# RWKV-7 and gated DeltaNet step: the right merge products of an item and the left ones of the next, at one place and in one PSUM bank

## The chip, the core and the metric

The kernel runs on one core of one Trainium2 chip. Five engines work side by side, each through its own queue in order: PE (TensorE, matrix products, with its weight loads shown apart as PEld), DVE (VectorE), ACT (ScalarE), POOL (GpSimd) and SP, which here only issues transfers. The metric is the time of one execution on the device in microseconds (us); lower is better. Before the change it is 2265.62 us, the median of three runs (2259.42 to 2267.38).

## The reference

One inference step of a trunk of two layers, for one prompt of 1024 tokens (16 learned tokens are put ahead of it) and eight samples of 8 tokens each: 1104 tokens of width 1024. The first layer is a gated DeltaNet, the second an RWKV-7 time mixing, which is what the change concerns:

```python
def rwkv_mixer(xn, S0, shift_prev, mu, w_rkvz, w0, w1, w2, a0, a1, a2, k_k, k_a, r_k, lnx_w, lnx_b, w_o):
    ...
    rkvz = jnp.einsum('sbtd,sde->sbte', xs[:4], w_rkvz)
    ...
    def step(S, inp):
        r_t, k_t, v_t, d_t, kk_t, b_t = inp
        S = (S * d_t[:, :, None, :]
             + jnp.einsum('bhvk,bhk->bhv', S, -kk_t)[..., None] * b_t[:, :, None, :]
             + v_t[..., None] * k_t[:, :, None, :])
        return S, jnp.einsum('bhvk,bhk->bhv', S, r_t)
    ...
    return y @ w_o, S, xn[:, -1]
```

The kernel does not go token by token. It takes chunks of 64 tokens, and what the tokens of a chunk do to each other becomes a triangular system of 64 x 64 for each chunk and head, whose inverse is worked out ahead of the recurrence.

## The kernel before

The program runs in this order: projections, convolution and recurrence of the first layer; its output projection; for the second layer the keys and decays; then the stage of this change (about 1520 to 1820 us of the profile), in which PE works out the projections r, v and z while the triangular inverses of all chunks are made beside it; and last the "wave", the RWKV recurrence over time with the output projection filled in.

**The projections** (`projections` in `layer1`) set the clock of the stage. They are 24 output tiles in segments of 384, 384 and 336 tokens. Each product of 128 x 128 weights (split in two, `whi` and `wlo`) with a stretch of tokens (`xa`, `xc`, `xh`, `xl`) goes into the PSUM tile `d`. After every 8 products the generator yields; one such step is called a tick here, u = 0, 1, 2 and so on. A finished tile is copied out by ACT (`ev`) and sent to memory (`rvd`, `zd`).

**The inverses** (`inverse_plan`). An item n (0 to 23) is a pair of heads in one of three segments, six chunks each. The items are taken in five groups b: 4, 5, 5, 5 and 5 of them. For an item:

- `prepare`: ACT forms two exponentials in the item's loaded tile `sldcak` (L62 on `sldcak`), DVE multiplies (L1321, L1327), POOL too (L1326). The next item's tile is loaded by SP (L1265); there are two such tiles, so a load waits until the item before has been used by `lower`.
- `lower`: PE makes 24 small products `fL` and 4 sums `frss`; ACT copies them to `sGD` (L1344) and `L` (L1346).

For a group, `chain` works on DVE: a transposition of `sGD` to `invA` (L1370), 31 steps of two instructions each (L1292 and L1294), which invert all 32 x 32 diagonal blocks at once, and two transpositions of the result, to `T1n` (L1377) and to `sTD` (L1378). Then the blocks are merged: for each item q of the group 12 left products give Y = (lower block) x `T1n` in PSUM (`mY`), ACT copies them to `invY` (two copies, L485), 12 right products give Y x `sTD` (`mU`), and ACT writes them with a minus sign back to `sTD` (two activations, L62). `store` sends the group's `sTD` to memory (`ttd`, L1393 and L1395). Both PSUM tiles carry the tag "m", of which there is one buffer, a bank: a new tile waits until the last one has been copied out.

**What sets the order.** Inside this stage PE's order is written out by hand: a table `plan` says which function runs at which tick. `lower` of item n stands at tick LOWER[n]; the five chains are pumped up to END[b]; item q of group b has its left products at END[b] + 4 + 4q and its right ones two ticks later; the store follows the last item. At one tick merges come before `lower`. The other engines' queues are ordered by the framework's scheduler from its own estimate of times, so that a change in PE's order can also move instructions on ACT, DVE, POOL and SP.

Of the kernel before, what the change touches and what calls it, by code (L numbers as in the profile page):

```python
# [10 lines left out]
AF = mybir.ActivationFunctionType  # L11
# [24 lines left out]
class Builder:  # L36
# [438 lines left out]

    def merge_left(self, L21, T1n, pool):

        p = self.ps("m", 1, "Y")
        v = p[:, 0:192].rearrange("p (c i) -> p c i", i=32)
        for c in range(6):  # L480
            for a in (0, 64):
                self.mm(v[a + 32:a + 64, c, :], L21[a:a + 32, c, :], T1n[a:a + 32, c, :])
        Y = self.t(pool, [128, 192], "invY", 2).rearrange("p (c i) -> p c i", i=32)
        for a in (32, 96):
            self.nc.scalar.copy(Y[a:a + 32], v[a:a + 32])  # L485
        return Y

    def merge_right(self, Y, TT):

        p = self.ps("m", 1, "U")  # L490
        v = p[:, 0:192].rearrange("p (c i) -> p c i", i=32)
        for c in range(6):
            for a in (0, 64):
                self.mm(v[a:a + 32, c, :], Y[a + 32:a + 64, c, :], TT[a + 32:a + 64, c, 0, :])
        for a in (0, 64):
            self.act(TT[a:a + 32, :, 1, :], v[a:a + 32], AF.Identity, scale=-1.0)

# [805 lines left out]
    def inverse_plan(self, pool):  # L1303

        nc, t = self.nc, self.t
        keep = {}
        GD, TD = self.GD, self.TD
# [72 lines left out]

        def left(b, q):
            C = slice(6 * q, 6 * q + 6)
            keep["Y", b, q] = self.merge_left(self.L21[b % 2][:, C], keep["T", b][:, C], pool)

        def right(b, q):
            self.merge_right(keep.pop(("Y", b, q)), TD[:, 6 * q:6 * q + 6])

# [8 lines left out]


        return prepare, lower, chain, left, right, store


# [521 lines left out]
    def layer1(self, ctx, right, stay, xa, xb, x):  # L1922

        nc, tc = self.nc, self.tc
        pool = lambda n, c: c.enter_context(tc.tile_pool(name=n, bufs=1, reuse_waits="tile"))
# [43 lines left out]
        ip = pool("rinv", ctx)  # L1969
        self.rwkv_masks(ip, True)  # L1970
        prepare, lower, chain, first_, second_, store = self.inverse_plan(ip)
        plan = {}
        at = lambda u, f, *a: plan.setdefault(u, []).append((f, a))
        LOWER = (13, 19, 25, 31, 35, 41, 47, 53, 59, 63, 69, 76, 82, 88, 92, 98, 104, 110, 116, 120, 126, 132, 137, 142)
        DUR, END = (0,), (52, 88, 112, 137, 164)
# [8 lines left out]
        for b in range(5):  # L1984
# [10 lines left out]
            for q in range(len(items)):  # L1995
                at(END[b] + 4 + 4 * q, first_, b, q)
                at(END[b] + 4 + 4 * q + 2, second_, b, q)
            at(END[b] + 4 + 4 * q + 1 + 2, store, b, items)
# [229 lines left out]
```

## Time and profile before

| | |
|---|---|
| median of three runs | 2265.62 us (2259.42 to 2267.38) |
| span of the profiled execution | 2250.2 us; the page gives no separate time for that execution |
| distance of the three times from that span | 9.2, 15.4 and 17.2 us |
| PE, PEld busy | 94%, 86% of the span |
| DVE, ACT, POOL busy | 69%, 57%, 41% |
| PE's granted clock, mean | 0.980 of full speed |
| merge products in the profile | 576 passes of `mY`, 576 of `mU`, first at 1566.4 us, last at 1817.4 us |
| copies behind them | 48 of 0.31 us (`invY`), 48 of 0.32 us (`sTD`) |

How to read the lines that follow: a row of the time order has the start in us from the span's start, the duration, the engine, the source line, the operation, out<-in, the shape and the count; in brackets stands how long the engine was idle before it and what ended that. `x24` behind 12 products is right, since each of them runs as two passes. PE's duration includes the time in which a product drains, so neighbouring products overlap, and the distance between two starts says what a product costs.

### The profile page before, as it was taken

The numbers are of one execution on the slowest core, as the hardware profiler recorded it, in microseconds if no ns is written. First come the engines' busy times: TensorE is split into PE (matmuls) and PEld (weight loads), VectorE is DVE, ScalarE is ACT, GpSimd is POOL, SyncE is SP. The second block draws the span as 40 slices with busy tenths as digits, with TensorE's granted clock in tenths as the row PEclk, the third lists the DMA queues.
The fourth block names the chain that finished last, engine by engine and source line by source line (L and its number), as shares of the span: only waits on it lengthen the run. The fifth ranks groups of instructions, "written<-read, shape, count | busy, mean of one in ns | idle before, by whom it ended". The sixth has DMA issues, their size and how long they took to land. (4 is left out here: it accounts for less than half of the span.)

```text
span 2250.2 us, 55173 instructions
## 1 busy us (share of the span) xinstructions
PE 2119.2 (94%) x20452; PEld 1933.2 (86%) x20452; DVE 1552.8 (69%) x4229; ACT 1272.4 (57%) x3641; POOL 915.7 (41%) x1253
## 2 busy tenths in 40 slices
PE   6999999999999999999999999989999999999997
PEld 5888898889898888989898999988888988888876
DVE  6778759586776859577434585766977647866755
ACT  5545556565555546556633365663745446677774
POOL 3444344453433435353323154343523344444444
PEclk9999999999999999999999999989999999999998
DMA  4333232433433233333516215645556376677754
GB/s 118 94 87 106 74 104 67 103 88 90 112 90 85 75 99 94 94 103 102 180 42 172 83 46 180 212 164 177 157 172 169 109 212 168 184 216 231 232 177 134
DMA packets 430662, 292.66 MB, mean 130 GB/s; under 512 B 147145, under 2 KB 412986, under 8 KB 430394
## 3 DMA queue, kind: packets, MB, share of 16 engines
q1 hardware_dynamic: 430394, 289.14, 44.8%
q8 instruction: 161, 2.64, 0.5%
q14 instruction: 107, 0.88, 0.1%
HBM read 197.68 MB, written 91.37 MB: 128 GB/s over the span
## 5 line engine op out<-in xcount | busy, mean ns | idle before, releaser
L90 POOL TENSOR_TENSOR wlo<-wraw,whi 128x512 fp32r<-128x512 f32 (+1 forms) x246 | 324.5, 1322 | 369.4 <-ACT whi L86 342.5
L76 PE MATMUL d<-xc,whi 128*128 128x384 f32 (+2 forms) x1006 | 282.5, 339 | 0.2 <-ACT whi L86 0.2
L86 ACT CAST whi<-wraw 128x512 fp32r<-128x512 f32 (+1 forms) x246 | 150.0, 613 | 132.4 <-PE dq L76 50.7
L435 DVE SCALAR_TENSOR_TENSOR cvy<-raw,cw,cvy 128x408 f32<-128x408 f32 (+2 forms) x288 | 180.5, 640 | 16.5 <-ACT cvy L62 14.6
L76 PEld LDWEIGHTS d<-xc,whi 128*128 128x128 f32 (+1 forms) x1006 | 183.7, 189 | 3.7 <-issue 1.4
L76 PE MATMUL d<-xc,wlo 128*128 128x384 f32 (+3 forms) x476 | 158.6, 342 | 2.2 <-POOL wlo L90 2.2
L76 PE MATMUL dz<-xc,whi 128*128 128x384 f32 (+1 forms) x480 | 149.3, 342 | 0.0
L76 PE MATMUL d<-xa,whi 128*128 128x384 f32 (+3 forms) x450 | 144.5, 345 | 3.7 <-ACT ev L2028 3.5
L76 PE MATMUL dv<-xc,whi 128*128 128x384 f32 (+1 forms) x480 | 146.7, 334 | 0.0
L835 POOL TENSOR_SCALAR Sb<-Sb,eglb 128x128 f32<-128x128 f32 x128 | 82.5, 663 | 87.7 <-DMA Sb<-in_state_gdn 51.2
L76 PE MATMUL dz<-xa,whi 128*128 128x384 f32 (+1 forms) x288 | 100.5, 349 | 0.0
L471 DVE TENSOR_TENSOR invtmp<-invA,invT 72x31 f32<-72x31 f32 (+15 forms) x248 | 95.5, 385 | 7.0 <-DMA invA<-ltd 4.2
L76 PE MATMUL dv<-xa,whi 128*128 128x384 f32 (+1 forms) x288 | 100.1, 348 | 0.1
L473 DVE TENSOR_TENSOR invT<-invT,invtmp 72x31 f32<-72x31 f32 (+15 forms) x248 | 96.9, 391 | 2.8
L76 PEld LDWEIGHTS d<-xc,wlo 128*128 128x128 f32 (+1 forms) x476 | 89.6, 190 | 6.2 <-POOL wlo L90 2.8
L76 PEld LDWEIGHTS d<-xa,whi 128*128 128x128 f32 (+1 forms) x450 | 85.4, 192 | 7.0 <-ACT ev L2028 3.8
L76 PEld LDWEIGHTS dz<-xc,whi 128*128 128x128 f32 x480 | 89.6, 192 | 0.8
L76 PEld LDWEIGHTS dv<-xc,whi 128*128 128x128 f32 x480 | 88.5, 188 | 0.5 <-issue 0.4
L62 ACT ACTIVATE o<-rA,gcol 128x128 f32<-128x128 f32 x128 | 46.6, 372 | 72.7 <-DVE S L746 72.1
L76 PE MATMUL d<-xa,wlo 128*128 128x384 f32 (+3 forms) x252 | 86.1, 342 | 1.1 <-POOL wlo L90 1.1
L62 ACT ACTIVATE attn<-attn,gcol 128x128 f32<-128x128 f32 x144 | 46.5, 390 | 71.1 <-POOL attn L546 71.0
L62 ACT ACTIVATE raw<-cvy 128x408 f32<-128x408 f32 (+2 forms) x96 | 47.3, 512 | 54.5 <-DVE cvy L435 53.6
(522 smaller groups left out, 7036.1 us busy)
## 6 DMA issues: line engine op xcount, KB each, us to landing
wraw<-in_gdn_w_in SPq DMA_DIRECT2D x96, 256.0 KB
wraw<-in_rwkv_w_rkvz SPq DMA_DIRECT2D x80, 256.0 KB
Sb<-in_state_gdn SPq DMA_DIRECT2D x64, 256.0 KB
sldcak<-cakd SPq DMA_DIRECT2D x24, 576.0 KB
wraw<-in_rwkv_w_o SPq DMA_DIRECT2D x42, 256.0 KB
E<-drow SPq DMA_DIRECT2D x24, 384.0 KB
attn<-drow SPq DMA_DIRECT2D x24, 384.0 KB
wraw<-in_gdn_w_out SPq DMA_DIRECT2D x36, 256.0 KB
```

The lines of the kernel that those rows point to most:

```text
L62: return self.nc.scalar.activation(out, in_, func, bias=bias, scale=scale, **kw)
L76: self.nc.tensor.matmul(out, lhsT, rhs, start=start, stop=stop)
L86: nc.scalar.copy(hi, x)
L90: e.tensor_tensor(lo, x, hi.bitcast(F32), op=ALU.subtract)
L435: nc.vector.scalar_tensor_tensor(y[:, 0:wd], raw[:, k:k + wd], cw[k], y[:, 0:wd], op0=ALU.mult, op1=ALU.add)
L471: nc.vector.tensor_tensor(tmp, A[:, j, j + 1:32].unsqueeze(2).broadcast_to([nb, n, m]), Tv[:, j, 0:m].unsqueeze(1).broadcast_to([nb, n, m] ...
L473: nc.vector.tensor_tensor(Tv[:, j + 1:32, 0:m], Tv[:, j + 1:32, 0:m], tmp, op=ALU.subtract)
L835: nc.gpsimd.tensor_scalar(Sb[:, u], Sb[:, u], self.eglb[:, hv, 4 * g + u:4 * g + u + 1], None, op0=ALU.mult)
```

## The change

The functions `left` and `right` of the plan become one function, `merges`, which stands at END[b] + 4 + 4q. It takes one PSUM tile (`mYU`), lets PE make the right products of item q - 1 and then the left products of item q into it, each on the partitions that it had before, copies `invY`, and last copies the right products to `sTD`. The first place of a group has only left products. The last right products keep their tick, two behind the last left ones, as does the store. A group of five items uses six PSUM tiles instead of ten.

```diff
-    def merge_left(self, L21, T1n, pool):
-
-        p = self.ps("m", 1, "Y")
-        v = p[:, 0:192].rearrange("p (c i) -> p c i", i=32)
+    def merge_view(self, p):
+
+        return p[:, 0:192].rearrange("p (c i) -> p c i", i=32)
+
+    def merge_left(self, L21, T1n, v, pool):
+
         for c in range(6):
             for a in (0, 64):
                 self.mm(v[a + 32:a + 64, c, :], L21[a:a + 32, c, :], T1n[a:a + 32, c, :])
...
-    def merge_right(self, Y, TT):
-
-        p = self.ps("m", 1, "U")
-        v = p[:, 0:192].rearrange("p (c i) -> p c i", i=32)
+    def merge_right(self, Y, TT, v):
+
         for c in range(6):
             for a in (0, 64):
                 self.mm(v[a:a + 32, c, :], Y[a + 32:a + 64, c, :], TT[a + 32:a + 64, c, 0, :])
-        for a in (0, 64):
-            self.act(TT[a:a + 32, :, 1, :], v[a:a + 32], AF.Identity, scale=-1.0)
+        return lambda: [self.act(TT[a:a + 32, :, 1, :], v[a:a + 32], AF.Identity, scale=-1.0) for a in (0, 64)]
...
-        def left(b, q):
-            C = slice(6 * q, 6 * q + 6)
-            keep["Y", b, q] = self.merge_left(self.L21[b % 2][:, C], keep["T", b][:, C], pool)
-
-        def right(b, q):
-            self.merge_right(keep.pop(("Y", b, q)), TD[:, 6 * q:6 * q + 6])
+        def merges(b, q, items):
+
+            v = self.merge_view(self.ps("m", 1, "YU"))
+            after = None
+            if q:
+                after = self.merge_right(keep.pop(("Y", b, q - 1)), TD[:, 6 * q - 6:6 * q], v)
+            if q < items:
+                C = slice(6 * q, 6 * q + 6)
+                keep["Y", b, q] = self.merge_left(self.L21[b % 2][:, C], keep["T", b][:, C], v, pool)
+            if after:
+                after()
...
             for q in range(len(items)):
-                at(END[b] + 4 + 4 * q, first_, b, q)
-                at(END[b] + 4 + 4 * q + 2, second_, b, q)
+                at(END[b] + 4 + 4 * q, merges, b, q, len(items))
+            at(END[b] + 4 + 4 * q + 2, merges, b, q + 1, len(items))
             at(END[b] + 4 + 4 * q + 1 + 2, store, b, items)
```

What it does to the order is seen on PE first, in group 0, between the first left products and the second ones. `d_19665` is the projection tile that PE is at, `frss` the end of `lower` of item 8. Before, with the rows from the last projection products ahead of the right products to the second left ones:

```order
L76 MATMUL d_19665<-xc_107,wlo_19549 128x384
L76 MATMUL d_19665<-xc_107,whi_19548 128x384 x2
L76 MATMUL mU_19682<-sTD_18465,invY_19662 32x32 x12
L76 MATMUL d_19665<-xc_107,wlo_19549 128x384
...
L76 MATMUL frss_19741<-ssq_19612,hones_17015 32x192 x4
L76 MATMUL d_19749<-xa_103,whi_19399 128x336
...
L76 MATMUL d_19749<-xc_107,wlo_19400 128x336
L76 MATMUL mY_19758<-T1n_19525,L_3276_18466 32x32 x12
```

and with the change:

```order
L76 MATMUL d_19665<-xc_107,wlo_19549 128x384
L76 MATMUL d_19665<-xc_107,whi_19548 128x384 x2
L76 MATMUL d_19665<-xc_107,wlo_19549 128x384
...
L76 MATMUL frss_19726<-ssq_19612,hones_17015 32x192 x4
L76 MATMUL d_19734<-xa_103,whi_19399 128x336
...
L76 MATMUL d_19734<-xc_107,wlo_19400 128x336
L76 MATMUL mYU_19743<-sTD_18465,invY_19662 32x32 x12
L76 MATMUL mYU_19743<-T1n_19525,L_3276_18466 32x32 x12
```

The right products of item 0 moved behind `lower` of item 8, to the left products of item 1. The same place on ACT, before:

```order
L485 COPY invY_19662<-mY_19649 32x192 x2
L62 ACTIVATE sTD_18465<-mU_19682 32x6x32 x2
L2028 COPY ev_19705<-d_19665 128x384
L1344 COPY sGD_18464<-fL_19713 128x32x6
L1346 COPY L_3277_18467<-fL_19713 32x192 x2
L62 ACTIVATE ssq_19778<-sldcak_19610 128x384
L485 COPY invY_19771<-mY_19758 32x192 x2
```

and with the change:

```order
L487 COPY invY_19662<-mYU_19649 32x192 x2
L2032 COPY ev_19690<-d_19665 128x384
L1343 COPY sGD_18464<-fL_19698 128x32x6
L1345 COPY L_3277_18467<-fL_19698 32x192 x2
L62 ACTIVATE ssq_19777<-sldcak_19610 128x384
L487 COPY invY_19768<-mYU_19743 32x192 x2
L62 ACTIVATE sTD_18465<-mYU_19743 32x6x32 x2
```

The two activations to `sTD` left the space between `invY` and `sGD` and now stand behind the next `invY`. In group 2, ACT ahead of and behind the second left products (`sldcak_21437`, with the change `sldcak_21430`, is the loaded tile of the same item), before:

```order
L62 ACTIVATE sldcak_21437<-sldcak_21437 128x383
L62 ACTIVATE sldcak_21437<-sldcak_21437 128x384
L62 ACTIVATE sTD_18465<-mU_21469 32x6x32 x2
L2028 COPY ev_21504<-d_21426 128x384
L485 COPY invY_21537<-mY_21524 32x192 x2
L1344 COPY sGD_18464<-fL_21546 128x32x6
```

and with the change:

```order
L62 ACTIVATE sldcak_21430<-sldcak_21430 128x383
L62 ACTIVATE sldcak_21430<-sldcak_21430 128x384
L2032 COPY ev_21482<-d_21419 128x384
L487 COPY invY_21527<-mYU_21502 32x192 x2
L62 ACTIVATE sTD_18465<-mYU_21502 32x6x32 x2
L1343 COPY sGD_18464<-fL_21538 128x32x6
```

The exponentials stay where they were; the copies of the first right products, which stood right behind them and ahead of the second left products' `invY`, now stand behind that `invY`, since their products moved there too. On DVE the steps of group 1's inverse and the token mixes (`mixs`) that run among them are interleaved in another order over some 90 rows; apart from that, DVE, POOL and SP change the places of single neighbouring rows. Behind this stage the order of all engines is as before.

4 lines of the change are left out of this document (2 added, 2 removed).

## The prediction

> **What bounds the kernel now.** I read the page first (TensorE, PE, is busy for 94% of the span), then the waits of PE between 1560 and 1830 us, the stretch in which the merges run, then the order of time around the longest of them, and last the busy time by stretch. "<- X" is what the wait ended with; the three numbers are us in total, times, longest us.
>
> ```profile
> PE 2119.2 (94%) x20452; PEld 1933.2 (86%) x20452; DVE 1552.8 (69%) x4229; ACT 1272.4 (57%) x3641; POOL 915.7 (41%) x1253
> ```
> ```profile
> PE mU L76 <- ACT invY L485: 4.0, 4, 2.5
> PE fL L76 <- DVE sldcak L1327: 3.6, 1, 3.6
> PE mY L76 <- ACT sTD L62: 2.8, 2, 2.1
> PE fL L76 <- issue: 2.2, 1, 2.2
> ```
> A right product (mU) waits 4.0 us in all for the copy of the left product (invY), a left product (mY) 2.8 us for the copy that frees the bank (sTD). These 6.8 us are what the change can reach. The other two, at fL, are waits for VectorE (DVE): they are where a faster PE would only wait longer.
>
> The longest merge wait, in order of time (start, us, engine):
>
> ```profile
> 1566.36 0.57 PE L76 MATMUL mY<-T1n,L 32*32 32x32 f32 x24
> 1566.86 0.45 PE L76 MATMUL d<-xa,whi 128*128 128x384 f32 x1
> 1570.15 1.08 ACT L62 ACTIVATE sldcak<-sldcak 128x383 f32<-128x383 f32 x2 [6.24 <-DVE sldcak L1327]
> 1571.75 0.63 ACT L485 COPY invY<-mY 32x192 f32<-32x192 f32 x2
> 1572.44 0.57 PE L76 MATMUL mU<-sTD,invY 32*32 32x32 f32 x24 [2.53 <-ACT invY L485]
> 1575.02 0.52 PE L76 MATMUL d<-xa,wlo 128*128 128x384 f32 x1
> 1575.34 0.52 PE L76 MATMUL d<-xa,whi 128*128 128x384 f32 x1
> 1575.79 1.03 PE L76 MATMUL fL<-sldcak 64*32 64x64 f32 x45
> 1575.90 0.48 ACT L2028 COPY ev<-d 128x384 f32<-128x384 f32 x1 [2.19 <-PE d L76]
> 1576.96 0.32 ACT L1344 COPY sGD<-fL 128x192 f32<-128x192 f32 x1 [0.59 <-PE fL L76]
> 1577.32 1.25 DVE L1370 STREAM_TRANSPOSE invA<-sGD 128x1024 f32<-128x1024 f32 x1 [6.06 <-ACT sGD L1344]
> ```
> The copy waits in ACT's queue behind an exponential that waits for DVE; the right product stands 16 projection products behind the left one, and PE is there first. After the wait the products start every 0.32 us. Behind them stands fL, and DVE has been idle for 6.06 us when fL's copy lets it begin the next chain. From there DVE is the bound (columns of the next fence: stretch, its length, then busy time of PE, PEld, DVE, ACT, POOL, then PE's clock):
>
> ```profile
> 1572.93:1577.14 4.21, 4.21 (x71) 3.46 (x65) 0.00 (x0) 1.30 (x4) 0.00 (x0) 0.60 0.05 18
> 1577.00:1641.00 64.00, 56.77 (x718) 50.97 (x712) 61.68 (x128) 48.80 (x119) 34.79 (x36) 1.00 0.55 166
> 1715.00:1740.00 25.00, 22.82 (x314) 20.58 (x312) 21.84 (x44) 16.87 (x43) 9.62 (x12) 1.00 0.68 160
> 1744.00:1785.00 41.00, 41.00 (x417) 38.44 (x416) 35.96 (x89) 21.50 (x52) 17.17 (x14) 1.00 0.33 102
> ```
> ```profile
> 1641.31 1.35 PE L76 MATMUL fL<-sldcak 64*32 64x64 f32 x45 [3.59 <-DVE sldcak L1327]
> ```
> From 1577 to 1641 DVE is busy for 61.68 of 64 us and PE then waits 3.59 us for it; from 1744 on PE has no gap.
>
> **The change part by part.** It adds and removes no product and no copy: 24 items with 12 left and 12 right products each (the profile counts two passes to a product, 24 to a group), and four copies to an item. It does three things.
>
> *It gives each copy four ticks instead of two* (a tick is 8 projection products). A right product of every item but a group's last now stands 32 products behind its left one, and the bank is needed again after as long.
>
> *It removes stops.* A quiet stop of the last group:
>
> ```profile
> 1809.29 0.52 PE L76 MATMUL d<-xc,whi 128*128 128x384 f32 x2
> 1809.64 0.34 PE L76 MATMUL d<-xc,wlo 128*128 128x384 f32 x1
> 1809.82 0.33 PE L76 MATMUL d<-xc,whi 128*128 128x384 f32 x1
> 1810.08 0.57 PE L76 MATMUL mU<-sTD,invY 32*32 32x32 f32 x24
> 1810.58 0.44 PE L76 MATMUL d<-xc,whi 128*128 128x384 f32 x1
> 1810.86 0.33 PE L76 MATMUL d<-xc,wlo 128*128 128x384 f32 x1
> ```
> From 1809.82 to 1810.86 are two steps of d, 0.175 each when undisturbed (two products from 1809.29 to 1809.64), and the stop: 1.04 - 0.35 = 0.69 us. A second group of 24 passes behind the first costs at most 0.50 (1810.08 to 1810.58) and at least 0.40 (the row's 0.57 less its last pass of 0.19, over 23 steps, times 24). So a removed stop saves 0.19 to 0.29; I take 0.24, the middle. Counted in the order of work, places where fL stands at the same tick counted once, groups 0, 1 and 2 lose 3 stops each, groups 3 and 4 lose 4 each.
>
> *It moves the copies on ACT* into fours (two invY, two sTD). These are the same 1.28 us, and the next stop asks for them 5.6 us (32 x 0.175) later.
>
> Term 1, group 0. Without mU at 1572.44, fL comes after 24 products: 1566.86 + 0.10 (the first step is longer, as at 1810.58) + 24 x 0.175 + 0.09 = 1571.25 instead of 1575.79, 4.5 us earlier. On ACT invY still ends at 1572.38, a copy of d (0.48) follows, then sGD at 1572.86: 4.1 us earlier than 1576.96. DVE is free by then, so its chain begins 4.1 us earlier, and being 96% busy it reaches L1327 and fL at 1641.31 4.1 us earlier. What PE gains besides in group 0 (0.83 at 1590.94, below, and 3 stops) only lengthens the wait at 1641: nothing. **4.1 us.**
>
> The clock bears on this term: the granted clock was 0.60 in the 4.2 us behind a wait of 2.53 us, which made 8 products cost 8 x (0.32 - 0.175) = 1.2 us more. The Trainium skill (TensorE: Matmul & The Clock Gate, Part 1) has the clock halve after an idle window of about 3.4 us; by it a wait of 2.5 us would cost nothing further, term 1 would be 1.2 smaller and the whole about 8.9. The trace shows the slow products, so the row decides.
>
> The other waits that fall away:
>
> ```profile
> 1590.94 0.57 PE L76 MATMUL mU<-sTD,invY 32*32 32x32 f32 x24 [0.83 <-ACT invY L485]
> 1662.07 0.57 PE L76 MATMUL mU<-sTD,invY 32*32 32x32 f32 x24 [0.54 <-ACT invY L485]
> 1694.79 1.08 ACT L62 ACTIVATE sldcak<-sldcak 128x383 f32<-128x383 f32 x2 [5.02 <-DMA sldcak<-cakd]
> 1696.61 0.57 PE L76 MATMUL mY<-T1n,L 32*32 32x32 f32 x24 [2.09 <-ACT sTD L62]
> 1705.13 0.57 PE L76 MATMUL mY<-T1n,L 32*32 32x32 f32 x24 [0.69 <-ACT sTD L62]
> ```
> Term 2, group 1: 0.54 + 3 x 0.24 = **1.3 us**; DVE is not what PE waits for between 1642 and 1696.
>
> Term 3, group 2: 2.09 + 0.69 + 3 x 0.24 = 3.5 us on PE. The wait at 1696.61 is ACT held for 5.02 us by a load; with the change the bank was freed before it. But PE then meets DVE again:
>
> ```profile
> 1703.64 0.56 DVE L1321 TENSOR_TENSOR sldcak<-sldcak 128x383 f32<-128x383 f32 x1 [0.71 <-ACT sldcak L62]
> 1712.49 0.56 DVE L1327 TENSOR_TENSOR sldcak<-sldcak 128x384 f32<-128x384 f32 x1 [0.26 <-POOL sldcak L1326]
> 1715.18 0.56 DVE L1321 TENSOR_TENSOR sldcak<-sldcak 128x383 f32<-128x383 f32 x1 [1.34 <-ACT sldcak L62]
> 1740.20 1.35 PE L76 MATMUL fL<-sldcak 64*32 64x64 f32 x45 [2.23 <-issue]
> ```
> DVE's idle time on that way, which an earlier fL (through the load that fL releases) can close, is 0.71 + 0.26 + 1.34 = 2.3 us up to 1715, and behind it at most the 25 - 21.84 = 3.2 us of the window. So between 2.3 and 3.5 come through; I take **3.0 us**.
>
> Term 4, groups 3 and 4: 8 x 0.24 = 1.9 us, less what the last inverse holds back:
>
> ```profile
> 1782.68 2.11 DVE L1377 STREAM_TRANSPOSE T1n<-invT 128x1024 f32<-128x1024 f32 x1
> 1785.60 0.57 PE L76 MATMUL mY<-T1n,L 32*32 32x32 f32 x24
> ```
> T1n ends at 1784.79, 0.8 us ahead of mY; group 3's four stops bring PE 0.96 earlier. DVE has 5 us of idle time in that window and follows in part; I take off 0.2. **1.7 us.**
>
> Sum: 4.1 + 1.3 + 3.0 + 1.7 = 10.1. The profiled span would go from 2250.2 to about 2240. The three times lie 9.2 to 17.2 above the span, their median 15.4; that distance does not change. Forecast: 2265.6 - 10 = **2255.6 us**. What follows after 1820 begins with loads and products that these stops release, so I carry the 10 us to the end whole.
>
> **The rivals.**
>
> *Bank held too long (slower).* A group's last right product still stands 16 products behind the last left one, and now it also asks for the bank, which waits for two sTD copies more. If these copies end later than 2.8 us (16 x 0.175) after the stop, PE waits there, and it decides if it is as at 1572.44: 2.53 + 1.2 of slow clock + some 0.2, 3.9 us, in five groups 19.5. Less the 10: 2275. The tightest such place:
>
> ```profile
> 1596.86 0.63 ACT L485 COPY invY<-mY 32x192 f32<-32x192 f32 x2
> 1598.93 0.57 PE L76 MATMUL mU<-sTD,invY 32*32 32x32 f32 x24
> ```
> invY ends at 1597.49, two more copies at 1598.14, still 0.8 us early; and this place lies in DVE's stretch, where it costs nothing. Chance 0.05.
>
> *The stops save nothing.* Right products use the array's rows from 32 and 96, left ones from 0 and 64. If the array drains between them, the joint place costs two stops, and terms 2 to 4 lose 14 x 0.24 = 3.4: 2259. For it: every change from d to a group shows such a gap. Against it: within a group the passes already alternate between two row places in one bank, 0.0165 us apart. The Trainium skill (TensorEngine Tiling (Array Packing), Gotcha 1: PSUM Pressure) says that different row tiles cannot use one PSUM bank at once, which speaks for a wait between the two halves; the alternating passes do not show it. Chance 0.17.
>
> *DVE's stretch does not follow.* Its 128 rows lean on ACT (48.80 of 64 us busy), and the order of both is new there; four copies in a row can hold an operand of DVE for 0.65 us more at each of group 0's three joint places, and another interleaving of inverse and mixes can lose one more. Term 1 falls to about 1: 2258.7. Chance 0.16.
>
> *DVE follows further.* If it closes 4.5 instead of 3.0 us before 1740, PE's wait there falls from 2.23 + 3.5 - 3.0 = 2.7 to 1.2, and the slow clock behind it, 1.2 as above, goes too: 2265.6 - 12.8 = 2252.8. For it: 2.3 + 3.2 us of idle time. Against: part of that is DVE and ACT waiting for each other. Chance 0.17.
>
> *Nothing moves*, because the stretch is made up later in loads: 2265. Chance 0.05.
>
> **How the numbers follow.** The forecast holds 0.40, the rivals the other 0.60. Below 0.5% (11.3 us) this kernel's runs cannot tell a change from none; my 10 lies just under it. With some 3 us of spread on each case, beyond 11.3 lie 0.14 of the forecast's 0.40, 0.11 of the fourth rival's 0.17, and 0.05 of the two at 2259: faster 0.30. Slower by 0.5% is most of the first rival, 0.04, and chance at the last, 0.01: 0.05. Same: 0.65. The range reaches from the fourth rival less twice that spread to the last: 2247 to 2265.
>
> **What would show it.** No PE wait for invY or sTD above 0.3 us; fL of group 1's last item 4 to 4.5 us earlier after its left product, without slow products ahead of it; DVE's chain beginning 4 us earlier and PE's wait for L1327 at its end still 3 to 5 us; joint places of 0.9 to 1.0 us; from there to the end of the merges another 5 to 7 us. I am wrong if fL is early and DVE's stretch is longer by as much, if a group's last right product waits, or if the 10 us are there at 1820 and gone at the end.

## The result, and the profile after

The change takes the median from 2263.9 to 2249.08 us (six runs each; 2259.4 to 2269.5 before, 2235.5 to 2251.8 after). The ratio of the comparison is 0.9944, with a 95% interval of 0.992 to 0.9968 (the quotient of the two medians is 0.9935). A later comparison, of five rounds, gave 2259.87 and 2238.23 us, ratio 0.9912 (0.9884 to 0.994). Both intervals lie below 1, so the kernel became faster; only the second lies wholly beyond 0.5%. The forecast was 2255.6 us in a range of 2247 to 2265: the time is in the range, 6.5 us below the forecast, and both ratios are on the side of "faster by over 0.5%", which had a chance of 0.30.

What PE waits for between 1561 and 1840 us of the changed kernel (total us, times, longest us):

```profile
PE fL L76 <- issue: 3.5, 1, 3.5
PE d L76 <- ACT ev L2032: 2.1, 1, 2.1
PE mYU L76 <- ACT sTD L62: 1.7, 2, 1.5
PE d L76 <- ACT whi L86: 1.7, 1, 1.7
PE d L76 <- POOL wlo L90: 1.4, 2, 1.1
```

Of the 6.8 us of merge waits 1.7 are left (2.1 and 3.3 in two later profiles of this kernel); the wait for VectorE (DVE) at L1327 (now L1326) is gone in this profile, and PE waits for other things in that stretch instead. The place where term 1 of the prediction was to come from, in order of time:

```profile
1573.72 0.57 PE L76 MATMUL mYU<-T1n,L 32*32 32x32 f32 x24
1577.34 1.08 ACT L62 ACTIVATE sldcak<-sldcak 128x383 f32<-128x383 f32 x2 [6.15 <-DVE sldcak L1326]
1578.61 0.80 PE L76 MATMUL fL<-sldcak 64*32 64x64 f32 x45
1578.95 0.63 ACT L487 COPY invY<-mYU 32x192 f32<-32x192 f32 x2
1579.98 0.33 ACT L1343 COPY sGD<-fL 128x192 f32<-128x192 f32 x1
1580.34 1.25 DVE L1369 STREAM_TRANSPOSE invA<-sGD 128x1024 f32<-128x1024 f32 x1 [1.89 <-ACT sGD L1343]
```

ACT is held by DVE as before (6.15 us), so the copy invY is as late as it was, but PE no longer stands in front of it: fL comes 4.89 us after the first left product (9.43 before), and DVE begins its chain 6.62 us after it (10.96 before), 4.3 us earlier.

The starts themselves cannot be compared: the first left product stood at 1566.36 us before and stands at 1573.72 now, although no engine's order differs ahead of it. So the stage is measured from there. S is the time from the first left product to the first product zz of the last z tile, and it has four parts: to the first fL, to the fL at tick 92 (the end of DVE's stretch, 1641.31 before), to the last fL at tick 142 (1740.20 before), to zz. Busy time by stretch (length; PE, PEld, DVE, ACT, POOL; PE's granted clock; DMA) of the kernel before, parts 1 and 2 in one row, then 3 and 4:

```profile
1566.36:1641.31 74.95, 64.89 (x840) 58.11 (x841) 65.83 (x133) 52.11 (x127) 36.72 (x38) 0.98 0.53 160
1641.31:1740.20 98.89, 93.19 (x1384) 83.91 (x1385) 74.73 (x176) 52.04 (x132) 31.16 (x41) 0.98 0.60 170
1740.20:1824.70 84.50, 84.50 (x904) 78.44 (x905) 47.81 (x104) 39.93 (x96) 32.35 (x39) 0.98 0.39 116
```

and of the changed one:

```profile
1573.72:1644.89 71.17, 64.78 (x841) 58.69 (x840) 63.65 (x134) 50.98 (x125) 36.32 (x39) 0.95 0.56 168
1644.89:1737.84 92.95, 88.95 (x1391) 81.62 (x1386) 73.15 (x174) 52.72 (x135) 30.79 (x40) 0.99 0.64 181
1737.84:1820.26 82.42, 82.42 (x904) 78.62 (x905) 49.12 (x104) 40.22 (x96) 32.60 (x39) 0.96 0.41 120
```

The parts are 3.8, 5.9 and 2.1 us shorter, 11.8 in all (258.34 and 246.54). From zz to the end it is 425.5 before and 427.0 after. The three lengths ahead, in and behind the stage make up the span's difference: +7.4 - 11.8 + 1.5 = -2.9 (2250.2 to 2247.3).

### The profile page after: what moved, and what is told of

The parts are those of the page before. It is cut to its first block, busy times and chain, and to the rows that moved or that the text cites. A ratio compares the mean times of both kernels' runs of the same rounds, so it can differ in the third digit from the quotient of the medians.

```text
span 2247.3 us, 55153 instructions
## 1 busy us (share of the span) xinstructions
PE 2115.6 (94%) x20452; PEld 1935.5 (86%) x20452; DVE 1551.2 (69%) x4229; ACT 1271.5 (57%) x3641; POOL 911.7 (41%) x1253
## 4 chain that ended last, share of the span: by engine, by line
PE 57%; DVE 16%; DMA 9%; ACT 8%; issue 4%; POOL 4%; SPq 2%; DVEq 0%; POOLq 0%; ACTq 0%
PE d L76 20%; PE dz L76 5%; PE rA L76 4%; PE dk L76 4%; PE dq L76 3%; DMA attn<-drow 3%; DVE invT L473 2%; DVE invtmp L471 2%; PE rX L80 2%; DVE cvy L435 2%; PE fG L76 1%; POOL attn L545 1%; PE zo L76 1%; PE dv L76 1%; PE do L76 1%
## 5 line engine op out<-in xcount | busy, mean ns | idle before, releaser
L90 POOL TENSOR_TENSOR wlo<-wraw,whi 128x512 fp32r<-128x512 f32 (+1 forms) x246 | 324.6, 1323 | 365.4 <-ACT whi L86 329.9
L86 ACT CAST whi<-wraw 128x512 fp32r<-128x512 f32 (+1 forms) x246 | 150.2, 613 | 128.7 <-PE dq L76 50.5
L62 ACT ACTIVATE w<-rA,nbp 128x128 f32<-128x128 f32 x144 | 51.4, 367 | 49.5 <-PE rA L76 49.0
```

Of the source, the lines that this page charges most:

```text
L62: return self.nc.scalar.activation(out, in_, func, bias=bias, scale=scale, **kw)
L86: nc.scalar.copy(hi, x)
L90: e.tensor_tensor(lo, x, hi.bitcast(F32), op=ALU.subtract)
```

## The experiments

Three words are used throughout. A stop is a place where PE leaves the projection's 128 x 128 products for a group of small ones. A joint place is a stop at which the right products of one item and the left ones of the next stand together. The two sides are the left products (array rows from 0 and 64) and the right ones (rows from 32 and 96). Rivals and theories with a letter are those of the recorded expectations.

All profiles, the two above included, give this table (us; "start" is the first left product, "f1" the first fL; waits and clock follow at each run):

| run | start | to f1 | f1 to tick 92 | 92 to 142 | 142 to zz | S |
|---|---|---|---|---|---|---|
| before | 1566.4 | 9.4 | 65.5 | 98.9 | 84.5 | 258.3 |
| e1_before | 1562.9 | 7.8 | 65.3 | 101.4 | 84.5 | 258.9 |
| e4_before | 1565.8 | 9.6 | 65.9 | 103.6 | 84.5 | 263.7 |
| after | 1573.7 | 4.9 | 66.3 | 92.9 | 82.4 | 246.5 |
| e1_after | 1575.9 | 4.9 | 67.3 | 93.0 | 82.5 | 247.7 |
| e3_after | 1565.4 | 4.9 | 65.2 | 95.0 | 80.1 | 245.1 |
| e1_g0 | 1570.3 | 4.9 | 65.2 | 98.7 | 84.5 | 253.3 |
| e1_g34 | 1563.3 | 8.8 | 65.7 | 103.6 | 82.4 | 260.5 |
| e2_two_ticks | 1561.8 | 9.8 | 65.0 | 104.3 | 84.8 | 263.9 |
| e2_apart | 1565.5 | 4.9 | 66.3 | 101.0 | 85.5 | 257.7 |
| e2_turns | 1576.1 | 4.9 | 66.3 | 94.4 | 79.1 | 244.7 |
| e3_turns | 1563.6 | 4.9 | 65.5 | 94.5 | 80.6 | 245.5 |
| e2_dummy | 1564.8 | 4.9 | 66.3 | 96.4 | 85.7 | 253.3 |
| e3_v2t | 1565.0 | 4.9 | 64.8 | 96.8 | 78.7 | 245.3 |

(In e3_v2t the last fL stands at tick 145. The runs whose labels begin with e1 and e2 were executed once each.)

### Both kernels again

No edit. The question is which of the differences come back.

> The kernel before, once more, for a second profile. All lengths here are S, from the start of the first left product to the start of the first zz product, which was 258.3 us before and 246.5 us with the change in the first two profiles. Theory A (the change shortens the stage by a fixed amount, and what differs ahead of the stage is scatter): S 257.5 to 259, a PE wait of 2.2 to 2.8 us ahead of the first right product, 3 to 4 us for L1327 at the fL behind group 1's first left products, while the start of the stage may move by some 7 us. Rival B (the scatter lies in the stage too): S away from 258.3 by 3 us or more.

> The change, once more. Theory A: S 245.5 to 247.5, that is 11 to 13 us less than the kernel before in this same group of runs; no wait at that same fL, and some 3.5 us at the last fL. Rival B: S away from 246.5 by 3 us or more. If the time of the whole differs by more than S does, the rest is scatter ahead of or behind the stage.

> The kernel before against itself, in five rounds, as a measure of the comparison and for a third profile of the stage. If the whole's scatter is chance in each execution (the granted clock is 0.50 or 1.00 for some 4 us behind waits of the same length), the ratio is 1.000 with an interval of about 0.003 to either side, and S lies between 257.5 and 260. If an execution with the profile is apart from those without (both profiles of this kernel so far were at 2250 us, its other runs at 2248 to 2270), the profiled time is again at 2252 or below and the median of the others at 2258 or above. If S is 262 or more, the saving of 12 us in the stage was too small by the scatter of two profiles.

S came back within 0.6 us before and 1.1 after, 11.2 us apart; the start differed by 13.0 us (1562.9 and 1575.9) and the rest behind zz by 6.0 (426.2 and 432.1). Compared by those two executions alone, at 2249.67 and 2257.44 us, the change would look 8 us slower. In the third profile of the changed kernel the start was 1565.4, among those of the kernel before, and the span 2236.2: the late start of the first two is scatter. The third profile of the kernel before gave S = 263.7, outside the expected 257.5 to 260; all that is new is in part 3 (103.6), where the wait for sTD at tick 120 was 3.10 us instead of 2.09 and the mean granted clock 0.94 instead of 0.98:

```profile
1641.35:1744.99 103.64, 97.05 (x1384) 87.53 (x1385) 74.27 (x176) 52.04 (x132) 31.11 (x41) 0.94 0.57 161
```

So S before is 260.3 in the mean of three and after 246.5: 13.8 us, with a standard error of 1.8 from the spread of the six. The comparison of the kernel before with itself gave 0.9993 (0.9975 to 1.0012), as it should: 1 lies inside, and 0.5%, below which the prediction held that nothing can be told, lies outside. Its profiled execution was at 2254.19 us beside a median of 2253.12: an execution with a profile is not a faster one, as the first two (2248.0 and 2250.2 of span) let one think. In every run that gives both, time and span are 1.7 us apart.

A single execution says little about S. Of the four e2 kernels below, each executed once on one chip (the kernel before took 2256.43 us there), e2_dummy was the fastest at 2247.84 us with S 253.3, ahead of e2_apart (2250.39, S 257.7), e2_turns (2251.84, S 244.7) and e2_two_ticks (2252.81, S 263.9). The same holds for e1: e1_g0 took 2252.55 us and e1_g34 2255.06, and the kernel before 2270.35 in one execution beside them and 2249.67 in e1_before. So the runs below are read by their parts.

### Group 0 alone

```diff
-            for q in range(len(items)):
-                at(END[b] + 4 + 4 * q, merges, b, q, len(items))
-            at(END[b] + 4 + 4 * q + 2, merges, b, q + 1, len(items))
+            if b in (0,):
+                for q in range(len(items)):
+                    at(END[b] + 4 + 4 * q, merges, b, q, len(items))
+                at(END[b] + 4 + 4 * q + 2, merges, b, q + 1, len(items))
+            else:
+                for q in range(len(items)):
+                    at(END[b] + 4 + 4 * q, first_, b, q)
+                    at(END[b] + 4 + 4 * q + 2, second_, b, q)
```

`first_` and `second_` are the left and right products with a tile each, as before the change.

> The change in group 0 alone; groups 1 to 4 as before, with separate places and tiles. It moves the first right products behind the lower part of item 8 and removes 3 stops, all in the stretch that VectorE bounds. Theory A (the chain of group 1 starts 4 us earlier and carries that to the fL at its end): from the first left product to the first fL 4.9 instead of 9.4 us, to the fL at tick 92 71 instead of 75 us, S 254.3, 4 us less than before. Rival C (VectorE's stretch does not follow, and the gain in the full change came from elsewhere): S 257 to 258.3. Rival D (a wait in group 1 or 2 takes it back): 71 us at tick 92 and S still 256.5 or more.

The fL at tick 92 came 70.1 us after the first left product (71 expected; 73.1 to 75.5 in the three profiles before), and S was 253.3, 7.0 below the mean of before; 4.4 of these are in the parts that the edit touches. Parts 3 and 4 are those of the kernel before at its quickest (98.7 and 84.5, where it had 98.9 to 103.6 and 84.5). The gain at tick 92 is 3.0 to 5.4 us and is not taken back; rivals C and D are out. The middle column of the table says why it comes through: from the first fL, with which DVE's chain begins, to the fL at tick 92 it is 64.8 to 67.3 us in all fourteen profiles, whatever PE gained or lost between them. DVE sets this stretch, and what counts is when it begins. The ends of DVE's rows say the same: in thirteen of the fourteen profiles the fL at tick 92 starts 0.26 to 0.29 us after L1327 (L1326 and L1336 in edited kernels) has ended on its operand, whatever the profile names as the end of the wait; only in the first profile of the change does it come 0.76 us after, so there PE was the later of the two, by half a microsecond.

The wait at its end is another matter. It was 3.6 us in all three profiles before and in e1_g34; here it was 0.78, with the change 0, 2.36 and 0.78. PE lost that time earlier in the stretch, at projection products that wait for ACT (2.13 and 1.68 us in this run, 1.42 and 0.23 at the same places of the first profile before). As long as DVE comes last at tick 92, it does not matter where PE stands idle before.

### Groups 3 and 4 alone

The same edit with `if b in (3, 4):`.

> The change in groups 3 and 4 alone; groups 0 to 2 as before. No merge wait stood there, so it takes away eight stops and nothing else. Theory A (a stop costs 0.69 us alone and the second 24 passes behind the first only 0.295, so 0.395 is saved at each): S 258.3 - 8 x 0.395 = 255.1. Rival E (the prediction's 0.24 for a stop): 258.3 - 1.9 = 256.4. Rival F (the array drains between the right and the left products): 258.3.

S was 260.5, in the range of the kernel before: by the total the run says nothing, since part 3, which this kernel has unchanged, was 103.6 (98.9 to 103.6 before). The expectation had not reckoned with that scatter. Part 4, the only one that holds the eight stops, does answer: 82.40, against 84.48 to 84.52 before and 82.42 and 82.50 with the whole change.

```profile
1741.36:1823.76 82.40, 82.40 (x905) 78.59 (x905) 49.09 (x104) 40.30 (x96) 32.58 (x39) 0.97 0.41 120
```

The clock has to be taken off before the 2.1 us are divided by eight. A granted mean of 0.98 over 84.5 us is 0.02 x 84.5 = 1.7 us lost to a slower clock. The 0.97 here and the 0.96 of the first profile of the change are both 0.965 before rounding, 2.9 us lost; e1_after had 0.963, 3.1 us lost, and e3_after 1.00. At full clock part 4 is then an estimated 82.8 before, 79.5, 79.4 and 80.1 with the change and 79.5 here: 2.7 to 3.4 us for eight stops, 0.34 to 0.42 each. The rows at full clock give it without that estimate. Before, merges of group 4 start every 3.49 us (1810.08, 1813.57), 6.98 for two; with the change a joint place starts every 6.60:

```profile
1802.24 0.47 PE L76 MATMUL mYU<-sTD,invY 32*32 32x32 f32 x18
...
1808.57 0.34 PE L76 MATMUL d<-xh,whi 128*128 128x384 f32 x1
1808.84 0.47 PE L76 MATMUL mYU<-sTD,invY 32*32 32x32 f32 x18
1809.13 0.22 PE L76 MATMUL mYU<-T1n,L 32*32 32x32 f32 x2
...
1809.22 0.48 PE L76 MATMUL mYU<-T1n,L 32*32 32x32 f32 x19
1809.62 0.44 PE L76 MATMUL d<-xh,wlo 128*128 128x384 f32 x1
```

That is 0.38 us saved for a stop. Priced as the prediction priced its quiet stop, a joint place costs 0.98 us where two stops cost 2 x 0.69, which is 0.40. So theory A holds, not 0.24 (E), and not nothing (F). The left passes (T1n) begin at 1809.13, while the last right ones (sTD) are still being issued; the whole place takes 0.78 us from its first pass to the next d, where 24 passes alone take 0.50. The second 24 cost 0.28 us, 12 ns each.

### The form of the products, and the order in the place

One product of 128 x 128 weights between the two halves (its 32 columns are read by nothing; all else is computed as before):

```diff
+            if 0 < q < items:
+                self.mm(p[:, 192:224], self.ident, self.ident[:, 0:32])
```

> The change with one product of 128 x 128 weights and 32 columns, into columns of the bank that nothing reads, between the right and the left products of each of the 19 joint places. Theory A (a stop is the change between the 128 x 128 form and the 32 x 32 form): each place pays a second stop, 0.985 + 0.3 to 0.4 and some 0.1 to 0.2 for the product itself, 1.35 to 1.6 us; 16 places outside VectorE's stretch at 0.4 to 0.6, S 252 to 256. Rival I (the price of a stop hangs on the long products of 384 or 336 columns around it, not on the form): 1.05 to 1.2 us, S 247.5 to 249.5.

```profile
1784.43 0.34 PE L76 MATMUL d<-xh,whi 128*128 128x384 f32 x1
1784.69 0.57 PE L76 MATMUL mYU<-sTD,invY 32*32 32x32 f32 x24
1785.19 0.41 PE L76 MATMUL mYU<-ident 128*128 128x32 f32 x2
1785.53 0.57 PE L76 MATMUL mYU<-T1n,L 32*32 32x32 f32 x24
1786.03 0.45 PE L76 MATMUL d<-xh,wlo 128*128 128x384 f32 x1
```

From the first pass to the next d it is 1.34 us, as the sum 0.50 + 0.34 + 0.50 of separate steps: the left passes take 0.50 again instead of 0.28. S was 253.3, in the expected 252 to 256 (theory A). A short product of the large form is enough to bring the stop back; long ones of 384 columns are not needed for it, so rival I is out. The run does not tell apart whether the change of form costs the time or whether the large product only keeps the two sides from overlapping.

Right and left products by turns, two and two (the left products are issued by a function of c, which `merge_right` calls):

```diff
         for c in range(6):
             for a in (0, 64):
                 self.mm(v[a:a + 32, c, :], Y[a + 32:a + 64, c, :], TT[a + 32:a + 64, c, 0, :])
+            if also:
+                also(c)
```

> The change, but in a joint place the right and the left products take turns, two and two, instead of 12 right ones and then 12 left ones. Theory O (passes on different row places overlap in time; in the trace of the change some left passes start among the last right ones): a joint place costs no more than 0.985 us, perhaps 0.75 to 0.95, S 243.5 to 246.5. Rival F (two row places that write one bank wait for each other): every change of sides costs, a joint place 1.2 us or more, S 249 or more.

> Right and left products by turns, timed. A joint place took 0.55 us instead of 0.785 to the next projection product, and there are 19: 4.5 us, of which the three of group 0 go into VectorE's stretch and some into waits at the fL of ticks 92 and 142. S 244 to 246 (244.7 in the first look), 1.5 to 3 us below the change; ratio 0.0007 to 0.0013 below that of the change of the same rounds. If the waits take it all: the same as the change.

```profile
1790.28 0.34 PE L76 MATMUL d<-xh,whi 128*128 128x384 f32 x1
1790.55 0.22 PE L76 MATMUL mYU<-sTD,invY 32*32 32x32 f32 x2
1790.56 0.22 PE L76 MATMUL mYU<-T1n,L 32*32 32x32 f32 x2
...
1790.94 0.19 PE L76 MATMUL mYU<-sTD,invY 32*32 32x32 f32 x1
1790.96 0.21 PE L76 MATMUL mYU<-T1n,L 32*32 32x32 f32 x2
1791.10 0.45 PE L76 MATMUL d<-xh,wlo 128*128 128x384 f32 x1
```

48 passes on both sides take 0.55 us to the next d, almost as few as 24 on one side (0.50). So the sides run beside each other, in one bank, and theory O holds: S was 244.7 and 245.5. In time it came to nothing: 2238.34 us beside 2238.23 for the change in the same rounds (ratios 0.9913 and 0.9912 to the kernel before). Places that are 0.23 us shorter, 16 of them outside DVE's stretch, would be 3.7 us; part 4 shows some of it (79.1 and 80.6 beside 80.1 to 82.5), part 3 nothing (94.4 and 94.5 beside 92.9 to 95.0). There a wait for sTD (2.42 and 2.23 us) and the one at the last fL (2.58 and 2.76) stand in both profiles by turns. The last fL starts 0.10 us after DVE's L1336 has ended, as it does after L1327 in all three profiles before and after L1326 in all three of the change, though the profile prints "issue" for its wait. So DVE sets that place too, and a shorter joint place ahead of it lengthens the wait; how much of the 3.7 us goes that way was not tested.

### The stops without the time

Joint places two ticks apart instead of four:

```diff
-            for q in range(len(items)):
-                at(END[b] + 4 + 4 * q, merges, b, q, len(items))
-            at(END[b] + 4 + 4 * q + 2, merges, b, q + 1, len(items))
-            at(END[b] + 4 + 4 * q + 1 + 2, store, b, items)
+            for q in range(len(items) + 1):
+                at(END[b] + 4 + 2 * q, merges, b, q, len(items))
+            at(END[b] + 4 + 4 * (len(items) - 1) + 1 + 2, store, b, items)
```

> Joint places as in the change, but two ticks apart instead of four: 16 of the 17 stops are gone, and each copy has two ticks again. S is the time from the first left product to the first zz product (258.3 before, 246.5 with the change). Theory A (stops and time are two gains that add): the wait of some 2.5 us ahead of the first right products is back and the first fL comes 9.4 to 9.8 us after the first left product, so that term 1 is lost; S 258.3 - 16 x 0.395 = 252, between 250.5 and 254. Rival G (nearly all of the gain is the stops, two ticks do for the copies): 246 to 248. Rival H (nearly all is the time for the copies): 256 or more, with merge waits of 5 us or more in sum.

S was 263.9, beside 258.3 to 263.7 in the three profiles before: nothing is gained, with 16 stops fewer, and one profile does not show a loss either. Theory A, that stops and time add, is wrong here by 12 us, and G by more; H had the side right (256 or more, 5 us of merge waits), though it did not say why. The waits:

```profile
PE mYU L76 <- ACT sTD L62: 11.3, 5, 4.7
PE mYU L76 <- ACT invY L487: 2.7, 2, 2.4
```

These are 14.0 us of merge waits, twice those of before (6.8 to 7.7). The tile now holds the results of two groups of products and is free for the next place only after four copies instead of two. The longest, and what ACT did then:

```profile
1698.21 0.42 PE L76 MATMUL mYU<-sTD,invY 32*32 32x32 f32 x8 [4.73 <-ACT sTD L62]
```
```profile
1695.77 1.08 ACT L62 ACTIVATE sldcak<-sldcak 128x383 f32<-128x383 f32 x2 [6.81 <-DMA sldcak<-cakd]
1696.86 0.63 ACT L487 COPY invY<-mYU 32x192 f32<-32x192 f32 x2
1697.50 0.65 ACT L62 ACTIVATE sTD<-mYU 32x192 f32<-32x192 f32 x2
```

ACT's queue is held for 6.81 us by an exponential that waits for a load, and all four copies stand behind it. This is the prediction's first rival (the bank held too long): at two ticks it decides, at four it does not. In these runs, sharing the bank is worth something only together with the four ticks.

### The time without the stops

Right products one tick ahead of the next left ones, in one tile with them:

```diff
+        def rights(b, q):
+            v = keep["v"] = self.merge_view(self.ps("m", 1, "YU"))
+            self.merge_right(keep.pop(("Y", b, q)), TD[:, 6 * q:6 * q + 6], v)()
...
-            at(END[b] + 4 + 4 * q + 2, merges, b, q + 1, len(items))
+                late.append((END[b] + 4 + 4 * q + (3 if n != items[-1] else 2), rights, b, q))
```

(`merges` then takes that tile for the left products; the entries of `late` are put into the plan behind all others, so that `lower` comes first at tick 59. The `...` stands for code left out.)

> The other half: the right products stand one tick ahead of the next left ones, still in one tile with them, so the copies have three ticks and the bank is asked for no more often, but all 17 stops are there again. Theory A: no merge wait over 0.6 us, the first fL 4.9 us after the first left product; 14 stops outside VectorE's stretch at 0.395 come back, S 246.5 + 5.5 = 252, less what the wait at the last fL (3.5 us with the change) gives back of them, so 250 to 252.5. Rival E (0.24 for a stop): 246.5 + 3.4 = 249.9 or less, 248.5 to 250. Rival G: 256 or more.

S was 257.7, in the range of G alone, but not for G's reason. The left products, a tick behind the right ones in the same tile, wait for the right ones' copies:

```profile
1579.48 0.57 PE L76 MATMUL mYU<-sTD,invY 32*32 32x32 f32 x24
1584.60 0.57 PE L76 MATMUL mYU<-T1n,L 32*32 32x32 f32 x24 [2.96 <-ACT sTD L62]
```

6.9 us in seven such waits, 3.6 of them outside DVE's stretch. So this kernel does not have the time without the stops; it has new waits and the stops. 246.5 + 14 x 0.40 + 3.6 = 255.7 leaves 2 us open, within the scatter of part 3. A second bank for the merges would separate the two more cleanly; all eight PSUM banks are taken in this stage, and no run frees one.

### A next step that does not pay

By turns, the last `lower` moved to the joint place at tick 145, the last chain to 169, group 4's places two ticks apart:

```diff
-        LOWER = (... 120, 126, 132, 137, 142)
-        DUR, END = (0,), (52, 88, 112, 137, 164)
+        LOWER = (... 120, 126, 132, 137, 145)
+        DUR, END = (0,), (52, 88, 112, 137, 169)
...
+            d = 4 if b < 4 else 2
             for q in range(len(items)):
-                at(END[b] + 4 + 4 * q, merges, b, q, len(items))
+                at(END[b] + 4 + d * q, merges, b, q, len(items))
```

> By turns, and besides the lower part of the last item at tick 145 instead of 142, at a joint place, the last chain up to tick 169 and group 4's places two ticks apart from 173 on. The wait for VectorE at the last fL (3.5, 2.6 and 2.6 us so far) should fall to under 0.5 with the slow clock behind it (up to 2 us), and one stop (0.45) goes: S 240 to 242.5, ratio 0.0015 to 0.002 below that of the turns. Rival J (T1n of the last group is what is bound, and comes no earlier): a wait of 2 to 4 us ahead of group 4's first left products, S 244 to 246. Rival K (two ticks are too few for four copies, as in the run with all places two ticks apart): waits for sTD of 2 us or more in group 4, S 245 or more.

The wait at the last fL is gone, there is none for T1n and none over 0.5 us for sTD in group 4, so J and K are out; yet S was 245.3, and the median 2245.38 us (ratio 0.9944, 0.9923 to 0.9966), not better than the change. Right behind that fL stand two waits that nobody had named, of PE for the next weights:

```profile
1743.16 0.44 PE L76 MATMUL d<-xh,whi 128*128 128x384 f32 x1 [1.95 <-ACT whi L86]
1745.47 0.69 PE L76 MATMUL d<-xh,wlo 128*128 128x384 f32 x1 [1.87 <-POOL wlo L90]
```

That is 3.8 us for the 2.2 to 3.5 that went. L86 and L90 convert the weights on ACT and POOL; with DVE's product ready 2.94 us ahead of the last fL, they are what PE meets next, and the wait for DVE had hidden it.

## Why the prediction was right, and where its terms were off

What each part saved (us), as forecast, in the first pair of profiles, and between the means of three profiles before and three after:

| | predicted | first pair | three and three |
|---|---|---|---|
| to tick 92 (term 1) | 4.1 | 3.8 | 3.4 |
| 92 to 142 (terms 2 and 3) | 4.3 | 5.9 | 7.6 |
| 142 to zz (term 4) | 1.7 | 2.1 | 2.8 |
| sum | 10.1 | 11.8 | 13.8 |

**Term 1** held in its working: fL 4.5 us and the chain 4.3 us earlier in the first pair, and DVE's stretch 0.8 us longer. The rival in which the stretch does not follow would have left about 1. What the prediction had wrong is the sign to look for: PE's wait at the end of the stretch was to stay at 3 to 5 us and was 0, 2.36 and 0.78. PE's idle time moved to earlier products, which DVE's bound covers. The slow products after the first wait also vary: in e1_before, with a wait of 2.15 us at that place, the clock stayed at 1.00 and fL came after 7.8 us instead of 9.4. So the 1.2 us of slow products in term 1 held for two of the three profiles before; that the one read for the prediction was among them was luck.

**The price of a stop** failed: 0.19 to 0.29 us, from second passes at 0.40 to 0.50. They cost 0.28, so a stop saves 0.38 to 0.40, and the 14 stops of terms 2 to 4 are some 5.5 us instead of 3.4. This is the term that was mis-sized. The row on which the bound was built (24 passes of one side, 0.57) cannot show what two sides do together. The count of stops, 17, was right, as was the judgement that the bank does not keep the sides apart. The Trainium skill (TensorEngine Tiling (Array Packing), Gotcha 1: PSUM Pressure) has it that different row tiles cannot use one bank at once; here 48 passes by turns in one bank take 0.55 us where 24 take 0.50, so the measurement decides against it for sides that write different partitions. The joint place, forecast at 0.9 to 1.0 us from its first pass to the next d, took 0.78.

**Terms 2 and 3** were too small for three reasons. The six stops give 6 x 0.40 = 2.4 instead of 1.4. The merge waits of part 3 were 3.5, 4.0 and 3.8 us before and 0.2, 0 and 2.4 after, 2.9 less in the mean; the prediction had 3.3 of them, read from one execution. And the slower clock behind waits was left out there: by the granted means (0.983, 0.967, 0.940 before; 0.995, 0.977, 0.982 after) it cost an estimated 1.7, 3.3 and 6.2 us before and 0.5, 2.1 and 1.7 after, 2.3 less. The wait at the last fL, which term 3 let grow to 2.7, was 2.2 to 2.8 before and 3.5, 2.6 and 2.2 after, so 0.2 more: 2.4 + 2.9 + 2.3 - 0.2 = 7.4, of 7.6 measured. DVE, which sets the last fL in all six, thus followed nearly the whole way and not just 3.0 us of it. The fourth rival had that direction right, but its sign, a wait of only 1.2 us there, did not come. DVE's idle time as the prediction added it up (2.3 us, and at most 3.2 behind it) is not a bound.

**Term 4** is 8 x 0.40 = 3.2 at full clock, less what the clock took in the first pair. The 0.2 taken off for the last inverse did not show: no wait for T1n stands in the profile after.

**The first rival** was placed correctly, but its working was not right. The prediction had the copies at group 0's last right products end 0.8 us early; these products waited, 1.49, 2.11 and 0.87 us:

```profile
1601.66 0.22 PE L76 MATMUL mYU<-sTD,invY 32*32 32x32 f32 x2 [1.49 <-ACT sTD L62]
```

It cost nothing, as the prediction said of that place, since it lies in DVE's stretch. A waiting last right product was one of the prediction's signs of being wrong; it came, without the loss that it was to stand for. The sentence "no PE wait for invY or sTD above 0.3 us" was wrong there, and in e3_after also at tick 132 (2.39 us), where ACT stood 5.87 us behind a load. The change makes that wait rarer; it does not remove its cause.

**The way to the end.** The prediction carried its 10 us to the end whole. From zz on it was 423.0 to 426.2 us before and 425.7 to 432.1 after, 3.4 us more in the mean, 1.5 times the standard error (2.2). By the total that is open, but a part of it is in the traces. The order behind the stage is not as before, although the section on the change says so: a dozen or so rows of DVE stand elsewhere in the wave, in all three profiles of the change, while the three profiles of the kernel before agree with each other. At one of these places DVE ran, before,

```profile
1894.89 0.69 DVE L1701 TENSOR_TENSOR Sb<-Sb,drsw 128x512 f32<-128x512 f32 x1 [0.47 <-PE drsw L76]
1895.73 0.48 DVE L1613 BATCH_NORM_STATS2 bnst<-y 128x6 f32<-128x64 f32 x3
```

and with the change

```profile
1892.97 0.48 DVE L1617 BATCH_NORM_STATS2 bnst<-y 128x6 f32<-128x64 f32 x3 [1.30 <-ACT y L1608]
1893.64 0.68 DVE L1705 TENSOR_TENSOR Sb<-Sb,drsw 128x512 f32<-128x512 f32 x1
```

The update Sb now stands behind a wait for ACT, and PE waits 0.56 us for Sb. The row `gnm` of DVE, which comes back 24 times in the wave, measures what follows: from its first to its sixth execution it is 76.5, 76.6 and 76.5 us in the three profiles before and 78.9, 79.0 and 78.9 after. So 2.4 of the 13.8 us are lost again there, in every profile alike. That the moved rows are the reason is argued from their place; no run puts them back.

That leaves some 11.4 us. The first comparison's interval, 7.2 to 18.1 us, holds it; the later one's, 13.6 to 26.2 us, does not, so what else gains there is open. The forecast of 10 for the whole came closer than its parts deserve, as the stops and waits that it priced too low and the loss behind the stage that it put at nothing partly cancel; this is luck. The forecast's distance of 15.4 us between span and median was nothing fixed: it was that execution being 8 to 16 us faster than the three runs. It did no harm, since only the difference was carried over.

## What to carry to other kernels

Two kinds of work that wait for each other's copies can share one place and one PSUM tile, if the copies get the time of the longer distance: the pair saved 13.8 us in the stage here, the shared tile at half the distance nothing. Price a removed wait with the slow clock that may follow it, from more than one profile. Before moving one wait away, ask what stands next behind it: here it was once the projection's own weights. And compare the engines' orders behind the changed stage too: here 2.4 us went there.

## What the hardware showed that was not expected

**Passes on the two sides of the array overlap**, although they write one PSUM bank (on different partitions). 24 passes on one side take 0.50 us to the next large product, 24 + 24 on two sides one after the other 0.78, by turns 0.55, and with one 128 x 128 product between them 1.34.

**The clock behind a wait goes by a fixed grid, not by the wait alone.** In each of the fourteen traces every change of the granted clock, between 0.50 and 1.00, lies on one grid with steps of 3.413 us, to within 0.003 us. Where a wait lies on that grid decides what it costs. In e3_after PE is idle for 2.33 us of one step, in most of a wait of 1.64 us and a whole one of 1.11, and the next step is slow (rows by steps of the grid; PE's busy time is the first number behind the length, the clock is the number behind the five engines):

```profile
1613.04:1616.45 3.41, 1.08 (x4) 0.66 (x4) 3.41 (x6) 3.26 (x8) 1.69 (x2) 1.00 0.44 171
1616.45:1619.86 3.41, 3.41 (x61) 2.72 (x61) 3.38 (x7) 2.14 (x6) 2.82 (x3) 0.50 0.64 154
1619.86:1623.28 3.42, 3.42 (x21) 3.42 (x20) 3.39 (x12) 2.62 (x8) 1.25 (x2) 1.00 0.73 239
```

In e2_turns a longer wait, 2.58 us, is cut in two by a border of the grid, and the clock stays:

```profile
1736.82:1740.23 3.41, 2.31 (x35) 1.78 (x33) 3.20 (x3) 2.65 (x7) 3.08 (x3) 1.00 0.28 76
1740.23:1743.64 3.41, 1.94 (x61) 1.66 (x62) 3.22 (x6) 3.35 (x8) 1.95 (x3) 1.00 0.87 213
1743.64:1747.06 3.42, 3.42 (x22) 3.35 (x20) 3.42 (x5) 3.36 (x9) 1.59 (x3) 1.00 0.32 97
```

The fourteen traces have 1060 steps at full clock between 1545 and 1820 us. Behind all 33 in which PE was idle for 1.9 us or more the clock fell, behind 9 of the 13 with 1.6 to 1.9 us, and behind none of the 1014 with less. A slow step with PE busy throughout loses 1.7 us. The wait ahead of the first right products shows both cases: 2.53 us within one step in the profile before, and 2.15 us cut into 1.07 and 1.08 in e1_before, where the clock stayed. Where the grid lies against the program differs from execution to execution, and in that sense the cost of such a wait is chance; behind each of the 17 waits of 2.7 us or more a slow step came. The Trainium skill (TensorE: Matmul & The Clock Gate, Part 1) says that the clock is judged over windows of about 3.4 us that run freely, whatever the kernel does. That fits; but its rule of one whole idle window does not, as 1.9 idle us of a window were always enough.

**The whole scatters more than the stage.** Executions of one kernel on one chip differ by 18 us (2247.9 to 2266.1 in 17 runs of the kernel before); the first left product, with the same orders ahead of it, came between 1561.8 and 1576.1 us. A change of ten microseconds is better read from the stage than from the end.
